# The first modulation of a transformer block: from split matmuls over weight rows to plain fp32 matmuls over weight columns, with part of the columns on VectorE

## The chip, the cores and the metric

The kernel runs on one core of one Trainium2 chip. The metric is the device time of one execution in microseconds (us); a comparison uses the median of several runs. The engines are named as the profile names them: PE (TensorE, the matmul engine), PEld (its weight loads), DVE (VectorE), ACT (ScalarE), POOL (GpSimd), SP (the engine that issues most of the DMA transfers).

## The reference, cut to what matters

The network is two blocks, one behind the other, on 256 tokens of width 1024. The first block works on two token streams (the latent one, `x`, and a context one, `ctx`, 512 tokens in all) and its first step scales and shifts every channel by values that come from a condition vector, one for each stream:

```
mod_lat = split(silu(c) @ w_mod[i] + b_mod[i], 6)
mod_ctx = split(silu(c_ctx) @ w_mod[i] + b_mod[i], 6)
u_ctx = h_ctx * (1 + mod_ctx[1]) + mod_ctx[0]
u_lat = h_lat * (1 + mod_lat[1]) + mod_lat[0]
y_ctx, y_lat = mla_mixer(u_ctx, u_lat, ...)
```

For the first layer the shift (part 0) and the scale (part 1) are needed before anything else can be multiplied: a product of two vectors of 1024 values with a matrix of 1024 x 2048 fp32 weights, 8 MB. All other modulation columns are needed later.

## The kernel before, in words

The kernel is one long program; a scheduler fixes the order of instructions on each engine when it is built, and each engine then works through its own list in that order and waits where data or a buffer is missing. Products of full fp32 weights are made by `mm3`: each operand is cut by `split` (line 117) into a rounded part `hi` (a cast, ACT, line 122) and a rest `lo` (a subtraction, DVE, line 123), and three matmuls (lines 156 to 158) go over hi x hi, hi x lo and lo x hi.

`first_in` (line 575) is the first stage. ACT starts four transfers of token rows (`xin`, line 581). PE transposes them (line 588), ACT copies the result to `xraw` (line 589); this is the function `mid`. `mod_first` makes the scale and shift as columns `mods[1]` and `mods[0]`, channel by channel on the partitions. Four units u of 512 weight columns each arrive as two transfers of 1 MB (line 134), are cut into hi and lo, and are the moving operand of 16 matmuls of 512 columns, with the 4 columns of `c4` (the two condition vectors, hi and lo) stationary. The result lies in 4 rows; ACT copies it (line 252) and 4 tiny matmuls turn it into columns (line 254). Units 0 and 1 give the first half of shift and scale, units 2 and 3 the second; after units 1 and 3 `use(b, ...)` applies them to the channels k = 4b to 4b+3: two `tensor_scalar` on DVE (line 598), one for each stream, then `split` into `xh` and `xl`, the operand of everything that follows.

What follows is the attention's input projection: first the unit `kr` (24 matmuls of 512 columns, tile `g<-xh,hi` and its two partners, weights `in_mla_in_kr`), then three units `in_mla_in` (tiles `acc`). Its weights pass the same `split`, so the casts and subtractions of `kr` stand between those of `use(1)` in the lists of ACT and DVE.

The modulation columns that are needed later are made on DVE alone by `mod_tick` (line 269): `crow[s]` holds silu of a condition vector on all partitions, a tile `mraw` of 128 weight columns lies transposed, and one `scalar_tensor_tensor` with an accumulated sum (line 278) gives one column for one stream.

Buffers: `wr` has 2 buffers `raw`, the phase 3 more; `mraw` has 3; `u` has 2.

Of the kernel before, what the change touches and what calls it, by code (L numbers as in the profile page):

```python
# [8 lines left out]
F32 = mybir.dt.float32  # L9
F32R = mybir.dt.float32r  # L10
I32 = mybir.dt.int32
AF = mybir.ActivationFunctionType
ALU = mybir.AluOpType
AX = mybir.AxisListType

P = 128
D = 1024
KD = D // P
T = 256
# [11 lines left out]
class Net:  # L31
# [198 lines left out]
        nc.scalar.dma_start(self.lncol, a["ln_cols"])  # L230

    def mod_first(self, mid, use):
        nc = self.nc
        pm = self.gen()
        sel = self.ft([4, 2], "msel")
        nc.scalar.dma_start(sel, self.a["k_sel42"])
        c4 = self.ft([P, KD, 4], "c4", 1, F32R)
        self.split(self.cT, c4[:, :, 0:2], c4[:, :, 2:4], "v")
        mods = [self.cp.tile([P, KD, 2], F32, name=f"mod0{c}") for c in range(2)]
        for u in range(4):  # L240
            ps = self.gen()
            for hf in range(2):
                raw = self.ft([P, 4 * 512], "raw", 3) if hf else None
                for i, W in enumerate(self.wload(self.a["w_mod0"][u, :, 4 * hf:4 * hf + 4, :], 4, 512, raw=raw)):
                    for j in range(2):
                        k = 4 * hf + 2 * i + j
                        for p, w in enumerate(W):
                            nc.tensor.matmul(ps[0:4, :], c4[:, k, :], w[:, j, :], start=k + p == 0, stop=k + p == KD)
            if u == 0:
                mid()  # L250
            r = self.mp.tile([P, D], F32, tag="mraw", name=self.nm("mrow"), bufs=3)[0:4, 0:512]
            nc.scalar.copy(r, ps[0:4, :])
            for j in range(4):
                nc.tensor.matmul(pm[:, 8 * u + 2 * j:8 * u + 2 * j + 2], r[:, j * P:(j + 1) * P], sel,
                                 start=True, stop=True)
            ch, b = u % 2, u // 2
            m = mods[ch][:, 4 * b:4 * b + 4, :]
            nc.vector.tensor_tensor(m, pm[:, 8 * u:8 * u + 8].rearrange("p (k s) -> p k s", s=2),
                                    self.bmod[:, 0, ch, 4 * b:4 * b + 4].unsqueeze(2).to_broadcast([P, 4, 2]), ALU.add)
            if ch:  # L260
                nc.vector.tensor_scalar(m, m, 1.0, None, ALU.add)
                use(b, mods[1], mods[0])

    def mod_start(self, i, ch, streams=(0, 1)):
        m = self.cp.tile([P, KD, 2], F32, tag="modcol", name=self.nm("modcol"), bufs=8)
# [309 lines left out]
    def first_in(self):  # L575
        nc, a = self.nc, self.a
        with self.phase("l0a"):
            raw = self.ft([P, KD, 512], "xraw")
            xs = [self.ft([P, D], "xin", 4) for _ in range(4)]
            for s in range(4):  # L580
                nc.scalar.dma_start(xs[s], a["x" if s > 1 else "ctx"][(s % 2) * P:(s % 2) * P + P])

            def mid():
                for s in range(4):
                    for b in range(0, KD, 4):
                        pt = self.trp()
                        for j in range(4):
                            nc.tensor.transpose(pt[:, j * P:(j + 1) * P], xs[s][:, (b + j) * P:(b + j + 1) * P], self.ident)
                        nc.scalar.copy(raw[:, b:b + 4, s * P:(s + 1) * P], pt.rearrange("p (j t) -> p j t", j=4))

            xT = self.new_xT(512)

            def use(b, A, B):
                for k in range(4 * b, 4 * b + 4):
                    u = self.ft([P, 512], "u", 2)
                    for s in range(2):
                        sl = slice(256 * (1 - s), 256 * (1 - s) + 256)
                        nc.vector.tensor_scalar(u[:, sl], raw[:, k, sl], A[:, k, s:s + 1], B[:, k, s:s + 1],
                                                ALU.mult, ALU.add)
                    self.split(u, xT[0][:, k, :], xT[1][:, k, :])  # L600

            self.mod_first(mid, use)
        return xT

    def layer0(self, stk):
        nc, a = self.nc, self.a
        sid = [1, 1, 0, 0]
        xT = self.first_in()
        self.crow = [self.mp.tile([P, D], F32, name=f"crow{i}") for i in range(2)]
        for r, src in zip(self.crow, (a["c"][0], a["c_ctx"])):  # L610
            nc.scalar.dma_start(r, src.unsqueeze(0).to_broadcast([P, D]))
            nc.scalar.activation(r, r, AF.Silu)
        j2 = self.mod_start(0, 2)
        j3 = self.mod_start(0, 3)
        j45 = []
# [1029 lines left out]
def constants():  # L1645
    k = {}
# [4 lines left out]
    for lv in range(7):  # L1651
        b = 1 << lv
        m = (tt // (2 * b)) * 2 * b + b
# [5 lines left out]
    j = (t % 32)[:, None]  # L1659
    i = np.arange(32)[None, :]  # L1660
    for lv in range(5):
        b = 1 << lv
# [4 lines left out]
    ti = np.arange(32)[None, :]  # L1667
    k["k_gneg"] = np.concatenate([np.where(m, -60000.0, 0.0) for m in (tt < tp, tt > tp, ti < tp % 32, ti > tp % 32)]
                                 + [tp != tt], axis=1).astype(np.float32)
    k["k_sel42"] = np.tile(np.eye(2, dtype=np.float32), (2, 1))  # L1670
    k["k_bsel"] = (np.arange(64) % 32 >= 16).astype(np.float32)[:, None]
    f = (t % 32 < 16).astype(np.float32)
    k["k_pmask"] = np.ascontiguousarray(np.stack([f, 1.0 - f], axis=1))
# [2 lines left out]
    pm = np.zeros((P, P), np.float32)  # L1676
# [13 lines left out]
def kblocks(w, n):  # L1690
    w = np.asarray(w)
    lead = w.shape[:-2]
    k, f = w.shape[-2] // P, w.shape[-1] // n
    w = w.reshape(*lead, k, P, f, n)
    r = len(lead)
    return np.ascontiguousarray(np.moveaxis(w, (r + 2, r + 1, r), (r, r + 1, r + 2)))
# [23 lines left out]
def layout1(x):  # L1720
    o = {}
    c = np.stack([np.asarray(x["c"])[0], np.asarray(x["c_ctx"])])
# [3 lines left out]
    for n in ("ln1_g", "ln1_b", "ln2_g", "ln2_b", "mla_q_norm", "mla_kv_norm"):  # L1726
        o[n] = np.asarray(x[n])
    w = np.asarray(x["w_mod"])
    o["w_mod0"] = kblocks(w[0, :, :2 * D], 512)[[0, 2, 1, 3]]
    w = np.concatenate([w[0, :, 2 * D:], w[1]], axis=1).reshape(KD, P, 10, D)  # L1730
    o["w_modb"] = np.ascontiguousarray(w.reshape(D, 10, KD, P).transpose(1, 2, 3, 0))
    o["c"] = np.asarray(x["c"])
# [1 line left out]
    w = np.asarray(x["mla_w_in"])[0]  # L1734
    o["mla_in"] = kblocks(w[:, :768], 256)
    o["mla_in_kr"] = kblocks(np.concatenate([w[:, 768:], w[:, 768:]], axis=1), P)[0]
    w = np.asarray(x["mla_w_q_up"])[0].reshape(512, 8, 192)
    o["mla_q_nope"] = tblocks(w[:, :, :P].reshape(512, D), 4)
    o["mla_q_rope"] = tblocks(w[:, :, P:].reshape(512, 512), 4)[0]
    w = np.asarray(x["mla_w_kv_up"])[0].reshape(256, 8, 256)  # L1740
# [3 lines left out]
    w = np.asarray(x["w_ffn_in"])  # L1744
# [3 lines left out]
    w = np.asarray(x["w_ffn_out"])  # L1748
    o["w_ffd0"] = rblocks(w[0], 2)
    o["w_ffd1"] = rblocks(w[1], 2)  # L1750
    w = np.asarray(x["gdn_w_in"])[0]
# [87 lines left out]
```

## Time and profile before

| | before |
|---|---|
| median of 3 runs (lowest, highest) | 2515.39 us (2508.4, 2516.76) |
| profiled execution, first to last instruction (span) | 2511.5 us |
| profiled execution's own time outside the span | not listed apart; the span is 3.9 us below the runs' median |
| PE busy, share of the span | 2350.2 us, 94% |
| DVE busy | 1767.2 us, 70% |
| ACT busy | 1258.2 us, 50% |

The busy share of PE is that of its records: a matmul counts from start to modelled end. The stage of which the change is a part is only about the first 50 us; how it stands there must be read from that stage's own rows, not from these shares.

### The profile page before, as it was taken

To read this page: it belongs to the slowest core of one execution; us is meant where nothing else is said; L and a number is where in the kernel's file an instruction comes from. 1 tells how busy PE (TensorE), PEld (TensorE's weight loads), DVE (VectorE), ACT (ScalarE), POOL (GpSimd) and SP (SyncE) were. 2 spreads that over 40 slices of the span, in tenths; PEclk is the share of its full clock that TensorE was granted. 3 is DMA by queue.
4 is the path that set the end of the run, shared out by engine and by line. 5 is a ranking of instruction groups with operands and counts; after the bars stand their busy time and mean duration, and the time that the engine had idled before them with its cause. 6 is when DMAs were issued, how large, how long until landed. Compare 5 with 4: busy or idle time off the path is not lost.

```text
span 2511.5 us, 38451 instructions
## 1 busy us (share of the span) xinstructions
PE 2350.2 (94%) x14526; PEld 1934.9 (77%) x14526; DVE 1767.2 (70%) x3380; ACT 1258.2 (50%) x2644; POOL 198.2 (8%) x264
## 2 busy tenths in 40 slices
PE   7999999999788999879799999999999999999998
PEld 4978878878677878768688778767788788767886
DVE  6886898965679979886655755577655555687554
ACT  6475432222375575645444555564645554665553
POOL 0000500000221021111300000001000000001000
PEclk9999999999989989989899999998999999998999
DMA  8544266641122121221655555432555455414552
GB/s 301 194 140 167 99 211 208 224 141 51 58 80 77 35 69 34 81 88 45 231 195 174 166 193 173 167 124 66 189 183 185 155 174 191 139 56 135 185 185 100
DMA packets 93634, 356.12 MB, mean 142 GB/s; under 512 B 12264, under 2 KB 13448, under 8 KB 86664
## 3 DMA queue, kind: packets, MB, share of 16 engines
q1 hardware_dynamic: 88544, 343.91, 41.4%
q10 hardware_dynamic: 3592, 6.02, 0.7%
q0 software_dynamic: 1312, 3.74, 0.4%
q8 instruction: 114, 1.87, 0.3%
q14 instruction: 72, 0.59, 0.1%
HBM read 348.77 MB, written 3.67 MB: 140 GB/s over the span
## 4 chain that ended last, share of the span: by engine, by line
PE 72%; DVE 13%; ACT 6%; DMA 4%; issue 3%; POOL 2%; ACTq 0%; DVEq 0%; POOLq 0%; SPq 0%
PE g L156 12%; PE g L158 12%; PE g L157 12%; PE acc L156 8%; PE acc L158 8%; PE acc L157 8%; DVE lo L123 2%; ACT hi L122 1%; DVE cvy L762 1%; DMA raw<-in_w_gu 1%; POOL t L163 1%; PE t L1288 1%; PE g L494 1%; PE acc L1514 1%; PE acc L996 1%
## 5 line engine op out<-in xcount | busy, mean ns | idle before, releaser
L122 ACT CAST hi<-raw 128x512 fp32r<-128x512 f32 (+3 forms) x740 | 488.8, 700 | 477.7 <-PE g L157 116.5
L123 DVE TENSOR_TENSOR lo<-raw,hi 128x512 fp32r<-128x512 f32 (+3 forms) x740 | 561.5, 791 | 205.5 <-ACT hi L122 199.3
L156 PE MATMUL g<-hi,xh 128*128 128x512 f32 (+1 forms) x1120 | 421.4, 376 | 14.1 <-DVE hid L1280 6.5
L158 PE MATMUL g<-hi,xl 128*128 128x512 f32 (+1 forms) x1120 | 410.2, 366 | 6.1 <-DVE xl L1245 4.8
L157 PE MATMUL g<-lo,xh 128*128 128x512 f32 (+1 forms) x1120 | 410.8, 367 | 1.2 <-DVE lo L123 1.2
L156 PE MATMUL g<-xh,hi 128*128 128x512 f32 (+1 forms) x776 | 280.9, 362 | 4.7 <-ACT cvu L758 4.7
L158 PE MATMUL g<-xh,lo 128*128 128x512 f32 (+1 forms) x776 | 279.0, 360 | 1.4 <-DVE lo L123 1.4
L157 PE MATMUL g<-xl,hi 128*128 128x512 f32 (+1 forms) x776 | 279.4, 360 | 0.0
L156 PEld LDWEIGHTS g<-hi,xh 128*128 128x128 f32 x1120 | 213.1, 190 | 52.7 <-DVE hid L1280 8.8
L158 PEld LDWEIGHTS g<-hi,xl 128*128 128x128 f32 x1120 | 212.7, 190 | 44.9 <-DVE xl L1245 5.7
L157 PEld LDWEIGHTS g<-lo,xh 128*128 128x128 f32 x1120 | 213.2, 190 | 34.6 <-DVE lo L123 2.1
L156 PE MATMUL acc<-xh,hh 128*128 128x512 f32 x440 | 176.1, 400 | 3.3 <-ACT hh L122 3.3
L123 DVE TENSOR_TENSOR xl<-raw,xh 128x512 fp32r<-128x512 f32 (+1 forms) x223 | 153.1, 698 | 30.2 <-ACT xh L122 30.2
L157 PE MATMUL acc<-xl,hh 128*128 128x512 f32 x440 | 172.9, 393 | 0.0
L158 PE MATMUL acc<-xh,hl 128*128 128x512 f32 x440 | 172.8, 397 | 0.0
L156 PEld LDWEIGHTS g<-xh,hi 128*128 128x128 f32 x776 | 151.0, 195 | 25.2 <-ACT cvu L758 5.6
L158 PEld LDWEIGHTS g<-xh,lo 128*128 128x128 f32 x776 | 150.6, 194 | 20.9 <-DVE lo L123 1.6
L157 PEld LDWEIGHTS g<-xl,hi 128*128 128x128 f32 x776 | 150.9, 195 | 18.7
L158 PE MATMUL acc<-hi,xl 128*128 128x512 f32 (+2 forms) x432 | 158.5, 370 | 4.6 <-DVE xl L1245 3.3
L1280 DVE SCALAR_TENSOR_TENSOR hid<-g,t,hid 128x256 f32<-128x256 f32 (+1 forms) x96 | 44.3, 461 | 167.8 <-ACT hid L1279 167.6
L157 PE MATMUL acc<-lo,xh 128*128 128x512 f32 (+2 forms) x432 | 159.4, 371 | 2.1 <-DVE lo L123 2.1
L156 PE MATMUL acc<-hi,xh 128*128 128x512 f32 (+2 forms) x432 | 160.6, 376 | 0.2 <-ACT hi L122 0.2
(567 smaller groups left out, 4152.5 us busy)
## 6 DMA issues: line engine op xcount, KB each, us to landing
raw<-in_w_gu SPq DMA_DIRECT2D x220, 512.0 KB, 4.4
raw<-in_w_down SPq DMA_DIRECT2D x88, 512.0 KB, 4.4
mraw<-in_w_modb SPq DMA_DIRECT2D x80, 512.0 KB, 4.5
raw<-in_w_in SPq DMA_DIRECT2D x28, 512.0 KB, 4.0
raw<-in_w_ffg SPq DMA_DIRECT2D x11, 1024.0 KB, 5.0
raw<-in_w_ffu SPq DMA_DIRECT2D x11, 1024.0 KB, 4.9
raw<-in_w_ffd SPq DMA_DIRECT2D x11, 1024.0 KB, 4.8
raw<-in_w_ffd SPq DMA_DIRECT2D x22, 512.0 KB, 4.3
```

Source lines behind the costliest of these rows:

```text
L122: nc.scalar.copy(hi, src)
L123: self.tail = nc.vector.tensor_tensor(lo, src, hi.bitcast(F32), ALU.subtract).ins
L156: nc.tensor.matmul(out, lh, rh, start=start, stop=False)
L157: nc.tensor.matmul(out, lh, rl, start=False, stop=False)
L158: nc.tensor.matmul(out, ll, rh, start=False, stop=stop)
L163: self.pow = self.nc.gpsimd.tensor_tensor(dst, s, self.mhalf[:, 0:n], ALU.pow).ins
L494: nc.tensor.matmul(po[:, tt * P:(tt + 1) * P], v[:, j, h * P:(h + 1) * P], PT[:, j * P:(j + 1) * P], start=j == 0, stop=j == nk // P - 1)
L762: nc.vector.scalar_tensor_tensor(y, u[:, :, j:j + T], w[:, j:j + 1], y, ALU.mult, ALU.add)
L996: nc.tensor.matmul(py[:, vh * P:(vh + 1) * P], Mt[:, 4 * (4 * d + vh) + c, :], src[:, vh, :], start=True, stop=True)
L1280: nc.vector.scalar_tensor_tensor(h, v, r, h, ALU.mult, ALU.mult)
L1288: nc.tensor.transpose(pt[:, j * P:(j + 1) * P], hid[:, j * P:(j + 1) * P], self.ident)
L1514: nc.tensor.matmul(pcv[s][:, ct * P:(ct + 1) * P], self.upad[:, ct, s * P + j:s * P + j + P], dg, start=ct + j == 0, stop=False)
```

## The change

The same 2048 columns are made in two ways. All 1024 scale columns and the last 256 shift columns go to PE as five units of 256 columns (`on_pe`, 1 MB each): the fp32 weights, uncut, are the stationary operand, block by block of 128 x 128, and the moving operand is `cT`, 2 columns. The result is at once in columns, in one PSUM tile `pm`. The first 768 shift columns go to DVE as six tiles of 128 (`on_dve`, 0.5 MB each), in the way of `mod_tick`. For this `crow` is loaded and passed through silu at the start instead of after the stage. No `split` of these weights, no copy of rows and no tiny matmuls are left; `+1` and the bias become one instruction. In `use`, the stream s = 1 is now scaled on ACT instead of DVE.

```diff
     def mod_first(self, mid, use):
-        c4 = self.ft([P, KD, 4], "c4", 1, F32R)
-        self.split(self.cT, c4[:, :, 0:2], c4[:, :, 2:4], "v")
...
-        for u in range(4):
-            ps = self.gen()
-            for hf in range(2):
-                raw = self.ft([P, 4 * 512], "raw", 3) if hf else None
-                for i, W in enumerate(self.wload(self.a["w_mod0"][u, :, 4 * hf:4 * hf + 4, :], 4, 512, raw=raw)):
-                    for j in range(2):
-                        k = 4 * hf + 2 * i + j
-                        for p, w in enumerate(W):
-                            nc.tensor.matmul(ps[0:4, :], c4[:, k, :], w[:, j, :], start=k + p == 0, stop=k + p == KD)
...
+        self.crow = [self.mp.tile([P, D], F32, name=f"crow{i}") for i in range(2)]
+        for r, src in zip(self.crow, (a["c"][0], a["c_ctx"])):
+            nc.scalar.dma_start(r, src.unsqueeze(0).to_broadcast([P, D]))
+            nc.scalar.activation(r, r, AF.Silu)
+        pm = self.gen()[:, 0:4 * KD].rearrange("p (c k s) -> p c k s", c=2, k=KD)
...
+        def on_pe(u, ch, j0):
+            raw = self.ft([P, KD, T], "raw", 3) if u % 2 else self.wr.tile([P, KD, T], F32, tag="raw", name=self.nm("raw"))
+            nc.sync.dma_start(raw, a["w_mod0"][u])
+            for j in range(2):
+                for k in range(KD):
+                    nc.tensor.matmul(pm[:, ch, j0 + j, :], raw[:, k, j * P:(j + 1) * P], self.cT[:, k, :],
+                                     start=k == 0, stop=k == KD - 1)
+
+        def on_dve(j):
+            raw = self.mp.tile([P, D], F32, tag="mraw", name=self.nm("mraw"), bufs=3)
+            nc.sync.dma_start(raw, a["w_mods"][j])
+            for s in range(2):
+                junk = self.mp.tile([P, D], F32, tag="mjunk", name=self.nm("mjunk"), bufs=1)
+                nc.vector.scalar_tensor_tensor(junk, raw, 1.0, self.crow[s], ALU.mult, ALU.mult,
+                                               accum_out=mods[0][:, j, s:s + 1])
+
+        def add(b, ch, j0, j1):
...
+            nc.vector.scalar_tensor_tensor(mods[ch][:, sl, :], src, float(ch), bias, ALU.add, ALU.add)
+
+        on_pe(0, 1, 0)
+        on_dve(0)
+        on_dve(1)
+        mid()
+        on_pe(1, 1, 2)
+        on_dve(2)
+        on_dve(3)
+        add(0, 1, 0, 4)
+        add(0, 0, 0, 4)
+        use(0, mods[1], mods[0])
+        on_pe(2, 1, 4)
+        on_dve(4)
+        on_pe(3, 1, 6)
+        on_dve(5)
+        on_pe(4, 0, 6)
+        add(1, 1, 4, 8)
+        add(1, 0, 4, 6)
+        add(1, 0, 6, 8)
+        use(1, mods[1], mods[0])
```

and in `use`:

```diff
-                        nc.vector.tensor_scalar(u[:, sl], raw[:, k, sl], A[:, k, s:s + 1], B[:, k, s:s + 1],
-                                                ALU.mult, ALU.add)
+                        Ak, Bk = A[:, k, s:s + 1], B[:, k, s:s + 1]
+                        if s:
+                            nc.scalar.activation(u[:, sl], raw[:, k, sl], AF.Identity, bias=Bk, scale=Ak)
+                        else:
+                            nc.vector.tensor_scalar(u[:, sl], raw[:, k, sl], Ak, Bk, ALU.mult, ALU.add)
```

**PE's list.** Before, in the first stage (transposes at line 588, matmuls with moving `hi` and `lo` and the four stationary columns `c4` at line 248, which the rows call `c_15`, and the tiny matmuls at line 254), around the end of unit 0:

```order
L248 MATMUL g_126<-hi_151,c_15_121 4x512
L248 MATMUL g_126<-lo_152,c_15_121 4x512
L588 MATMUL t_175<-ident,xin_109 128x128 x4
L588 MATMUL t_181<-ident,xin_109 128x128 x4
L588 MATMUL t_187<-ident,xin_110 128x128 x4
L588 MATMUL t_193<-ident,xin_110 128x128 x4
L254 MATMUL g_118<-msel_119,mrow_211 128x2 x4
L248 MATMUL g_218<-hi_221,c_15_121 4x512
```

PE's list of the change from its first matmul to the unit `kr` (transposes now line 607, the new matmuls line 246):

```order
L607 MATMUL t_157<-ident,xin_108 128x128 x2
L246 MATMUL g_124<-csT,raw_127 128x2 x16
L607 MATMUL t_157<-ident,xin_108 128x128 x2
L607 MATMUL t_163<-ident,xin_108 128x128 x4
L246 MATMUL g_124<-csT,raw_205 128x2 x16
L607 MATMUL t_169<-ident,xin_109 128x128 x4
L607 MATMUL t_175<-ident,xin_109 128x128 x4
L607 MATMUL t_181<-ident,xin_110 128x128 x4
L607 MATMUL t_187<-ident,xin_110 128x128 x4
L246 MATMUL g_124<-csT,raw_257 128x2 x14
L607 MATMUL t_193<-ident,xin_111 128x128 x4
L607 MATMUL t_199<-ident,xin_111 128x128 x4
```

Behind these rows stand the last 2 matmuls of `raw_257`, 16 of `raw_281` and 16 of `raw_305`, and then `kr`. The 64 matmuls of 512 columns and the 16 tiny ones are gone, 80 matmuls of 2 columns have come.

**DVE's list.** Before, it begins with the cut of the condition vectors and then has the rests of the weights, in the order of their transfers:

```order
L120 CAST c_15_121<-csT 128x8x2
L123 TENSOR_TENSOR c_15_121<-csT,c_15_121 128x8x2
L123 TENSOR_TENSOR lo_130<-raw_127,hi_129 128x1024
L123 TENSOR_TENSOR lo_134<-raw_127,hi_133 128x1024
L123 TENSOR_TENSOR lo_148<-raw_145,hi_147 128x1024
```

In the change it begins with the addition of the bias to the first four scale columns, which PE makes from `raw_127` and `raw_205`; the sums over weights (line 254) stand behind it:

```order
L261 SCALAR_TENSOR_TENSOR mod_126<-g_124,bmod 128x8
L254 SCALAR_TENSOR_TENSOR mjunk_147,mod_125<-mraw_145,crow_118 128x1024
L254 SCALAR_TENSOR_TENSOR mjunk_149,mod_125<-mraw_145,crow_119 128x1024
L254 SCALAR_TENSOR_TENSOR mjunk_153,mod_125<-mraw_151,crow_118 128x1024
L254 SCALAR_TENSOR_TENSOR mjunk_155,mod_125<-mraw_151,crow_119 128x1024
L254 SCALAR_TENSOR_TENSOR mjunk_225,mod_125<-mraw_223,crow_118 128x1024
```

So all of DVE's work of the stage now stands behind PE's second unit. Further down DVE's list of the change, at the second `use` (line 261 adds, line 621 scales, line 123 cuts; `raw_366` is the weight of `kr`):

```order
L254 SCALAR_TENSOR_TENSOR mjunk_303,mod_125<-mraw_299,crow_119 128x1024
L261 SCALAR_TENSOR_TENSOR mod_126<-g_124,bmod 128x8
L261 SCALAR_TENSOR_TENSOR mod_125<-mod_125,bmod 128x4
L261 SCALAR_TENSOR_TENSOR mod_125<-g_124,bmod 128x4
L621 TENSOR_SCALAR u_326<-xraw_107,mod_126,mod_125 128x256
L621 TENSOR_SCALAR u_331<-xraw_107,mod_126,mod_125 128x256
L123 TENSOR_TENSOR lo_369<-raw_366,hi_368 128x1024
L123 TENSOR_TENSOR xl_117<-u_326,xh_116 128x512
```

The three additions read what PE made from `raw_257`, `raw_281` and `raw_305`; the cut of `kr`'s weight, which its third matmul needs, stands behind them.

## Rows read from the trace of the kernel before

**Rows 1.** The page's head.
```profile
span 2511.5 us, 38451 instructions
```

**Rows 2.** Windows: length, busy PE, PEld, DVE, ACT, POOL, granted clock, DMA share, GB/s.
```profile
10.00:20.00 10.00, 6.20 (x24) 3.17 (x25) 6.65 (x7) 6.27 (x8) 0.00 (x0) 1.00 1.02 421
...
60.00:80.00 20.00, 19.16 (x162) 18.96 (x161) 18.43 (x29) 7.00 (x16) 1.52 (x2) 1.00 0.64 211
```

**Rows 3.** PE's timeline: start, length, line, tiles, count [idle before, releaser].
```profile
13.80 1.94 PE L588 MATMUL t<-ident,xin 128*128 128x128 f32 x8 [13.80 <-DMA xin<-in_ctx]
15.39 0.78 PE L248 MATMUL g<-hi,c 128*4 128x512 f32 x1
...
21.50 1.15 PE L588 MATMUL t<-ident,xin 128*128 128x128 f32 x8 [0.24 <-ACT xraw L589]
...
45.57 0.79 PE L158 MATMUL g<-xh,lo 128*128 128x512 f32 x1 [1.43 <-DVE lo L123]
```

**Rows 4.** Groups of instructions from 0 to 52 us: busy, mean ns.
```profile
L123 DVE TENSOR_TENSOR lo<-raw,hi 128x1024 fp32r<-128x1024 f32 x19 | 22.5, 1218 | 9.8 <-ACT hi L122 9.8
L122 ACT CAST hi<-raw 128x1024 fp32r<-128x1024 f32 x19 | 18.8, 1045 | 4.3 <-issue 4.1 <-DMA raw<-in_w_mod 0.2
...
L248 PE MATMUL g<-lo,c 128*4 128x512 f32 x32 | 13.1, 408 | 0.3 <-DVE lo L123 0.3
...
L254 PE MATMUL g<-msel,mrow 4*128 4x2 f32 x32 | 4.2, 249 | 2.8 <-ACT mrow L252 2.8
```

**Rows 5.** A DMA list: the first `xin` transfer, issued at 2.15 us; last, landing time.
```profile
xin<-in_ctx ACTq DMA_DIRECT2D x1, 512.0 KB, 11.5
```

**Rows 6.** DVE's timeline around the second `use` and the first later column.
```profile
42.79 0.17 DVE L261 TENSOR_SCALAR mod<-mod 128x8 f32<-128x8 f32 x1
43.00 1.38 DVE L598 TENSOR_SCALAR u<-xraw,mod,mod 128x256 f32<-128x256 f32 x4
...
45.44 1.28 DVE L123 TENSOR_TENSOR xl<-u,xh 128x512 fp32r<-128x512 f32 x2
...
62.58 1.22 DVE L278 SCALAR_TENSOR_TENSOR mjunk<-mraw,crow 128x1024 f32<-128x1024 f32 x1
...
63.83 1.22 DVE L278 SCALAR_TENSOR_TENSOR mjunk<-mraw,crow 128x1024 f32<-128x1024 f32 x1
```

**Rows 7.** The only plain fp32 matmuls of 128x128 weights and 2 columns.
```profile
L916 PE MATMUL t<-ones,half 128*128 128x2 f32 x32 | 3.9, 236 | 0.0
```

**Rows 8.** PE's timeline of short matmuls in two later stretches.
```profile
1709.25 3.62 PE L1514 MATMUL acc<-cdg,upad 128*128 128x128 f32 x16
1712.66 2.58 PE L1562 MATMUL g<-sv,halfA 128*128 128x64 f32 x16
...
2249.95 1.91 PE L1562 MATMUL g<-sv,halfA 128*128 128x64 f32 x16
2251.70 1.06 PE L1574 MATMUL g<-gv,gla_AT 128*128 128x64 f32 x8
```

**Rows 9.** PEld's timeline (weight loads) of the first of these stretches.
```profile
1712.45 1.75 PEld L1562 LDWEIGHTS g<-sv,halfA 128*128 128x128 f32 x8
```

**Rows 10.** Windows as in group 2, of four later stretches and the restart at 45 us.
```profile
894.90:911.90 17.00, 17.00 (x304) 12.47 (x304) 13.42 (x21) 7.93 (x14) 0.73 (x1) 0.50 0.11 34
1707.20:1714.10 6.90, 6.90 (x81) 6.66 (x81) 6.66 (x11) 4.30 (x17) 1.49 (x4) 0.51 0.01 2
1720.70:1724.10 3.40, 3.40 (x147) 2.65 (x133) 2.65 (x6) 1.31 (x6) 1.10 (x2) 1.00 0.02 5
1724.30:1731.10 6.80, 6.80 (x31) 6.09 (x30) 6.62 (x11) 1.18 (x7) 0.73 (x1) 0.50 0.27 82
45.00:51.70 6.70, 6.13 (x14) 4.79 (x15) 6.70 (x12) 2.22 (x4) 0.00 (x0) 0.50 0.56 195
```

**Rows 11.** PE's timeline: what stands in the first and third stretch of group 10.
```profile
894.23 0.44 PE L1116 MATMUL acc<-big,Mt 32*32 32x32 f32 x16 [1.16 <-DVE Mt L944]
...
1720.37 0.52 PE L1528 MATMUL g<-m_E 32*32 32x32 f32 x38
```

More of the change, by code (lines that the diff above doesn't have):

```diff
@@ L232, in mod_first @@
     def mod_first(self, mid, use):
[L233 to L236, printed above, removed]
-        c4 = self.ft([P, KD, 4], "c4", 1, F32R)
-        self.split(self.cT, c4[:, :, 0:2], c4[:, :, 2:4], "v")
-        mods = [self.cp.tile([P, KD, 2], F32, name=f"mod0{c}") for c in range(2)]
-        for u in range(4):
-            ps = self.gen()
-            for hf in range(2):
-                raw = self.ft([P, 4 * 512], "raw", 3) if hf else None
-                for i, W in enumerate(self.wload(self.a["w_mod0"][u, :, 4 * hf:4 * hf + 4, :], 4, 512, raw=raw)):
-                    for j in range(2):
-                        k = 4 * hf + 2 * i + j
-                        for p, w in enumerate(W):
-                            nc.tensor.matmul(ps[0:4, :], c4[:, k, :], w[:, j, :], start=k + p == 0, stop=k + p == KD)
[L249 to L262, printed above, removed]
@@ new lines, in mod_first @@
+        nc, a = self.nc, self.a
+        self.crow = [self.mp.tile([P, D], F32, name=f"crow{i}") for i in range(2)]
[3 more added lines that the diff above has]
+        pm = self.gen()[:, 0:4 * KD].rearrange("p (c k s) -> p c k s", c=2, k=KD)
+        mods = [self.cp.tile([P, KD, 2], F32, name=f"mod0{c}") for c in range(2)]
+        def on_pe(u, ch, j0):
[5 more added lines that the diff above has]
+                                     start=k == 0, stop=k == KD - 1)
@@ new lines, in on_dve @@
+        def on_dve(j):
[6 more added lines that the diff above has]
+        def add(b, ch, j0, j1):
+            sl = slice(j0, j1)
+            bias = self.bmod[:, 0, ch, sl].unsqueeze(2).to_broadcast([P, j1 - j0, 2])
+            src = pm[:, ch, sl, :] if ch or j0 == 6 else mods[0][:, sl, :]
+            nc.vector.scalar_tensor_tensor(mods[ch][:, sl, :], src, float(ch), bias, ALU.add, ALU.add)
@@ L608, in layer0 @@
         xT = self.first_in()
[L609 to L612, printed above, removed]
         j2 = self.mod_start(0, 2)
@@ L1669, in constants @@
                                  + [tp != tt], axis=1).astype(np.float32)
-    k["k_sel42"] = np.tile(np.eye(2, dtype=np.float32), (2, 1))
     k["k_bsel"] = (np.arange(64) % 32 >= 16).astype(np.float32)[:, None]
@@ L1728, in layout1 @@
     w = np.asarray(x["w_mod"])
-    o["w_mod0"] = kblocks(w[0, :, :2 * D], 512)[[0, 2, 1, 3]]
+    o["w_mod0"] = kblocks(np.concatenate([w[0, :, D:2 * D], w[0, :, D - 256:D]], axis=1), 256)
+    o["w_mods"] = np.ascontiguousarray(w[0, :, :D - 256].T.reshape(6, P, D))
     w = np.concatenate([w[0, :, 2 * D:], w[1]], axis=1).reshape(KD, P, 10, D)
```

## The prediction

> **What bounds the kernel now.** I read the page first, for the span [rows 1], then the windows, to see how full PE is once the network proper runs: 19.16 of 20 us between 60 and 80 us, and it stays so [rows 2]. From there on PE is the bound, and whatever moves the start of that dense work moves the end by the same amount. So the question is when the dense work begins. In PE's timeline that is the third matmul of `kr`, at 45.57 us, released by DVE's cut of `kr`'s weight; the two matmuls ahead of it are done by then, and behind it PE does not wait again for long [rows 3]. Next I read the groups of the first 52 us to see what fills them: on ACT and DVE the casts and subtractions of the weights, 1.045 and 1.218 us each, 19 of each, of which 16 are of `w_mod` [rows 4]. DVE is the last link before the restart: it adds the bias, scales, and then cuts `kr`'s weight [rows 6]. Of PE the reader should see that it is fed and not full in this stage, and that its moving operand is wide, 512 columns.
>
> **What the change removes.** On ACT 16 casts, 16.7 us, and on DVE 16 subtractions, 19.5 us [rows 4]. On PE 64 matmuls of 512 columns (0.41 us each in their records) and the 16 tiny ones [rows 4]. That these 16 stand as 32 in the row shows that a plain fp32 matmul is two instructions on PE; line 916 shows the same for the form that is now added [rows 4, 7].
>
> **What it adds on PE.** 80 matmuls of 128x128 weights and 2 columns are thus 160 pairs of weight load and matmul, beside the 32 transposes as before: 192 instructions one behind the other. What one costs is the disputed price. With few columns the weight load sets the pace: 16 with 64 columns start 1.75 us before the next group at the full clock, 0.109 us each [rows 8], and 32 with 2 columns were busy 3.9 us, 0.122 each [rows 7]. At the low clock (granted 0.51, [rows 10]) 16 with 128 columns take from 1709.25 to 1712.66, 0.213 each [rows 8], and with 64 columns the loads still stand about 0.22 apart (8 in 1.75 us, [rows 9]): fewer columns save nothing, and the load slows with the clock. [...]
>
> [...]
>
> **Which clock.** PE begins cold: the first 8 transposes start 1.59 us before the matmul that follows them, 0.20 us each, which is the slow pace (the granted clock reads as full there, the pace does not) [rows 3]. Before, the 512-column matmuls behind them soon run at the full clock. In the change there is no wide matmul until `kr`. [...] From 894.9 to 911.9 us PE was busy 17.00 of 17.00 us, with many 32x32 matmuls between wide ones, and stayed at 0.50 the whole time; from 1720.7 to 1724.1 it was busy throughout with such small ones at the full clock, and the next stretch was granted 0.50 [rows 10, 11]. A full PE list is thus not enough. Against this, the clock came back at 1714.1 out of matmuls of 128 and 64 columns at the slow pace [rows 8, 10]. [...]
>
> [...]
>
> **The sum.** PE's first instruction waits for the first `xin`, issued at 2.15 us and landed 11.5 us later; PE began at 13.80 [rows 3, 5]. In the change SP's list has 2 MB instead of 3 ahead of or beside it, because the second and third transfers are 0.5 MB; at 421 GB/s [rows 2] that is 2.4 us less, 11.4. Bounds 11.3 and 13.8; I take 12.0. PE's list then needs 40.9 us, and some waits for ACT's copies between transposes, as the 0.24 us before [rows 3]: three of them, 0.7 us (bounds 0 and 1.5). PE is through at 53.6 us. Behind it on DVE wait three additions at 0.17, two scalings at 0.35 (four in 1.38) and the cut of `kr`'s weight, 1.22 [rows 4, 6]: 2.4 us, so the third matmul of `kr` can start at 56.0 instead of 45.57: **10.4 us later**. By the bounds 9.0 to 13.1.
>
> The restart itself I take as costing the same: before, PE ran at 0.50 from 45.0 to 51.7 us [rows 10]; in the change it also comes out of the low clock. If that lasts some 3 us less, 1.5 us come back. The sum on the profiled span is 2511.5 + 10.4 = 2521.9; the runs' median lies 3.9 us above this span, and on it the forecast is 2515.4 + 10.4 = **2526 us**.
>
> **What is hidden.** DVE's list begins with an addition that waits for PE's second unit: 72 instructions, 15.3 us, so 27.3 us. From there 12 sums at 1.25 (62.58 to 63.83) are 15.0, and with the first `use` (four scalings 1.4, four cuts 2.6) and two additions DVE is ready at 46.7, 6.9 us before PE [rows 6]. If that cover goes, DVE sets the end; see the first rival. `crow` is the fifth and sixth transfer in ACT's queue: with 3 MB there and at most 5.5 MB of weights beside it, 8.5 MB at 421 GB/s [rows 2] end at about 23 us, 1 us for silu, before the 27.3 at which DVE asks. The scaling that moves to ACT and the ACT time freed lie beside DVE. `mraw` is held by the sums, so SP's later transfers wait for DVE, but the last weight for PE (`raw_305`) goes out after the fourth sum, about 32 us, 14 us before PE comes to it. `in_mla_in` goes out when PE lets go of the `wr` buffer, about 53.6, while `kr` still needs 24 matmuls.
>
> **Rival 1, not slower: the short matmuls run at the full pace.** Its place is PE's list, its price 192 x 0.109 to 0.122 instead of 0.213, and it decides below a mean of 0.198 us, where the delay falls under 7.5 us. Then PE is through at about 35 us and DVE sets the end. Its list begins between 20.3 us (PE's second unit) and 25 (`crow`), say 22.5; 15.0 for the sums, 4.2 for additions and the first `use`, 2.4 for the rest: the cut of `kr` ends at 44.1, 1.5 us earlier than before. Time 2514, between 2512 and 2516.5. For it: line 916's row; against it: the 17 us at 0.50.
>
> **Rival 2: the delay is given back later.** The work behind the stage would have to have slack. PE had 0.84 us of it in 60 to 80 us, DVE 1.57 [rows 2]: taken off the 10.4 they leave 8.0, time 2523.4, and off the lower bound of 9.0 they leave 6.6, time 2522, within 0.3%. Low-clock stretches further down, such as that of 6.8 us [rows 10], can also fall otherwise; one more or less is some 3 us either way.
>
> **Rival 3: PE starts late and waits more.** With 13.8 us and 1.5 us of waits the delay is 13.1, time 2528.5, and one more slow stretch makes 2531.
>
> **Faster** by over 0.3% (7.5 us, about what runs of this kernel can tell from no change) would need DVE's list to begin at 16.5 us, ahead of PE's second unit even at the full clock; only later stretches could do it.
>
> **The numbers.** The slow clock holds the stage: 0.84, of which 0.71 come out above 7.5 us and 0.13 below, for rivals 2 and 3 and the bounds. Rival 1: 0.12, nearly all of it within 0.3%. What is left, 0.04, goes to either side. Slower 0.71, within 0.3% 0.25, faster 0.04. The likeliest case's own range is 2521 to 2530; with rival 1 taken in as far as 2 in 10 demand it is 2514 to 2531.
>
> **What would show it.** After: the groups of line 246 with 160 records; their starts 0.21 us apart (right) or 0.11 (wrong: rival 1); the third matmul of `kr` near 56 us, released by DVE's cut, and DVE waiting for PE ahead of the second `use`. If DVE runs up to that point without a wait, or waits there for `crow` or `mraw`, the hidden part was misjudged. If the start is late as forecast and the end is not, rival 2 holds.

## The result, and the profile after the change

The changed kernel takes 2536.33 us (median; 2525.58 to 2540.72 over 5 runs) against 2515.39 us (2508.4 to 2524.05 over 5 runs) before: ratio 1.0072, 95% interval 1.0051 to 1.0092, which is 18 us slower, between 13 and 23. The forecast of 2526 us had the direction and too small a size; the median lies 5 us above the range's upper end. The profiled execution is the shortest of its runs, 1.8 us outside its span:

```profile
span 2523.8 us, 38569 instructions
```

Against the 2511.5 us of [rows 1] its span is 12.3 us longer. First the stage itself, in PE's timeline (columns as in [rows 3]; line 607 are the transposes, line 246 the new matmuls, lines 156 to 158 `kr`):

```profile
10.85 0.66 PE L607 MATMUL t<-ident,xin 128*128 128x128 f32 x2 [10.85 <-DMA xin<-in_ctx]
11.30 6.83 PE L246 MATMUL g<-csT,raw 128*128 128x2 f32 x32
17.98 1.52 PE L607 MATMUL t<-ident,xin 128*128 128x128 f32 x6
19.30 6.83 PE L246 MATMUL g<-csT,raw 128*128 128x2 f32 x32
25.98 3.74 PE L607 MATMUL t<-ident,xin 128*128 128x128 f32 x16
29.51 3.35 PE L246 MATMUL g<-csT,raw 128*128 128x2 f32 x28
32.72 1.46 PE L607 MATMUL t<-ident,xin 128*128 128x128 f32 x8
33.98 14.51 PE L246 MATMUL g<-csT,raw 128*128 128x2 f32 x68
48.34 0.78 PE L156 MATMUL g<-xh,hi 128*128 128x512 f32 x1
48.91 0.63 PE L157 MATMUL g<-xl,hi 128*128 128x512 f32 x1
50.72 0.80 PE L158 MATMUL g<-xh,lo 128*128 128x512 f32 x1 [1.18 <-DVE lo L123]
```

PE works without a gap from 10.85 to 48.34 us. The first two groups of 32 records take 6.68 us from their start to the next group, 0.21 each, and so do the last 68; only the 28 that begin at 29.51, behind 16 transposes, run at 0.115. The third matmul of `kr` starts at 50.72, 5.15 us later than in [rows 3]. DVE's timeline (sums at line 254, additions at 261) says who is late:

```profile
26.16 0.17 DVE L261 SCALAR_TENSOR_TENSOR mod<-g,bmod 128x8 f32<-128x8 f32 x1 [26.16 <-PE g L246]
...
43.67 1.22 DVE L254 SCALAR_TENSOR_TENSOR mjunk<-mraw,crow 128x1024 f32<-128x1024 f32 x1
48.52 0.17 DVE L261 SCALAR_TENSOR_TENSOR mod<-g,bmod 128x8 f32<-128x8 f32 x1 [3.63 <-PE g L246]
...
49.45 1.22 DVE L123 TENSOR_TENSOR lo<-raw,hi 128x1024 fp32r<-128x1024 f32 x1
```

It starts when PE's second unit is done, is through with its sums at 44.9, stands 3.63 us for PE, and needs 2.4 us from there to the cut of `kr`'s weight. The windows (as in [rows 2, 10]) show the low clock from the middle of the stage into `kr`, and the dense work behind it as full as before:

```profile
60.00:80.00 20.00, 19.11 (x160) 18.90 (x159) 17.07 (x25) 5.69 (x13) 1.22 (x2) 1.00 0.75 267
33.30:53.70 20.40, 19.23 (x82) 17.95 (x81) 16.67 (x36) 11.19 (x20) 0.00 (x0) 0.50 0.72 265
```

Of the low clock only 3 us lie behind `kr`'s third matmul, where before they were 6, so `kr`'s last matmul starts at 56.99 for 53.72, and behind it the dense work is 4.0 us late. That is a third of the 12.3 us by which the profiled span grew. The order of the instructions behind the stage is the same in both kernels, so each can be laid beside its partner; the delay of PE's starts (median over 50 us of the run) against the kernel before is my own reckoning from the two traces:

```
at us of before     60    300   600   850   1150  2500
changed kernel      4.0   5.2   7.8   13.2  17.3  12.5
```

So two thirds of this execution's loss arise far behind the change. What waits there is seen in PE's waits from 780 to 1260 us that end in nothing the profile names (us in total, times, longest). Before:

```profile
PE acc L1116 <- issue: 0.6, 1, 0.6
PE t L1116 <- issue: 0.5, 1, 0.5
PE g L1116 <- issue: 0.2, 1, 0.2
```

After (line 1134 is the line 1116 of before):

```profile
PE acc L1134 <- issue: 5.4, 3, 2.5
PE acc L158 <- issue: 2.6, 1, 2.6
```

1.3 us have become 8.0. These stand in stretches of 32x32 matmuls, some 10 ns apart.

### The profile page after: what moved, and what is told of

It reads as the page before. It is cut to its first block, busy times and chain, and to the rows that moved or that the text cites. A ratio compares the mean times of both kernels' runs of the same rounds, so it can differ in the third digit from the quotient of the medians.

```text
span 2523.8 us, 38569 instructions
## 1 busy us (share of the span) xinstructions
PE 2360.8 (94%) x14590; PEld 1957.3 (78%) x14590; DVE 1759.8 (70%) x3377; ACT 1245.6 (49%) x2632; POOL 197.1 (8%) x264
## 4 chain that ended last, share of the span: by engine, by line
PE 72%; DVE 13%; ACT 6%; DMA 4%; issue 3%; POOL 2%; ACTq 0%; DVEq 0%; POOLq 0%; SPq 0%
PE g L156 12%; PE g L157 12%; PE g L158 12%; PE acc L156 8%; PE acc L157 7%; PE acc L158 7%; DVE lo L123 2%; ACT hi L122 1%; DMA raw<-in_w_gu 1%; PE g L246 1%; DVE cvy L780 1%; POOL t L163 1%; DMA raw<-in_w_ffg 1%; PE t L1306 1%; PE g L513 1%
## 5 line engine op out<-in xcount | busy, mean ns | idle before, releaser
L122 ACT CAST hi<-raw 128x512 fp32r<-128x512 f32 (+3 forms) x724 | 472.9, 693 | 466.7 <-PE g L157 111.7
L123 DVE TENSOR_TENSOR lo<-raw,hi 128x512 fp32r<-128x512 f32 (+3 forms) x724 | 542.5, 783 | 192.7 <-ACT hi L122 186.4
```

Source lines behind the costliest of these rows:

```text
L122: nc.scalar.copy(hi, src)
L123: self.tail = nc.vector.tensor_tensor(lo, src, hi.bitcast(F32), ALU.subtract).ins
```

## The experiments

**Theory 1**: the start is late, and the shifted run loses more behind it, by low-clock stretches that fall otherwise. **Theory 2**: a late start costs its delay and no more; the rest is chance of single runs. The first four kernels set them against each other; all shared the runs of the kernel before (median 2516.47 us).

**The changed kernel again**, no edit. 

> The changed kernel once more, nothing edited. Its first profile put the third matmul of kr 5.15 us later than before (50.72 for 45.57 us), while the medians differ by 20.9 us; about 12 us of the profiled execution's loss arise behind the stage. Theory 1 (the later loss belongs to the change, because all that follows runs shifted and the low-clock stretches fall otherwise): again 15 to 21 us over the kernel before, and in a second trace the delay against before grows at the same places, near 800 and 1140 us. Theory 2 (5 us from the stage, the rest chance of the runs): 4 to 12 us this time, and the low-clock stretches of the second trace lie otherwise than in the first.

Measured: 2532.35 us, ratio 1.0056 (1.0037 to 1.0075). The loss is real, and its second trace is worse in the stage:

```profile
29.63 5.97 PE L246 MATMUL g<-csT,raw 128*128 128x2 f32 x28
...
51.58 0.77 PE L156 MATMUL g<-xh,hi 128*128 128x512 f32 x1
...
53.95 0.80 PE L158 MATMUL g<-xh,lo 128*128 128x512 f32 x1 [1.18 <-DVE lo L123]
```

The 28 records that were fast in the first trace are slow here: 40.6 us from 10.96 to 51.58 for 192 instructions, 0.21 each throughout; `kr` is 8.4 us late. The issue waits are there again, in the same places:

```profile
PE acc L1134 <- issue: 6.0, 3, 2.5
PE acc L158 <- issue: 2.3, 1, 2.3
```

**A pure delay**, the kernel before with

```diff
                 nc.vector.tensor_scalar(m, m, 1.0, None, ALU.add)
+                if u == 3:
+                    late = self.acc1()
+                    for i in range(28):
+                        nc.tensor.matmul(late[:, 2 * i:2 * i + 2], self.ident, m[:, 3, :], start=True, stop=True)
```

> The kernel before with a pure delay: 28 plain fp32 matmuls of the identity with 2 columns (56 instructions, their result not read) on PE ahead of kr, nothing else moved. The third matmul of kr comes 4 to 6 us later. Theory 1 (a late start of the dense work brings further losses behind it): 12 to 20 us slower than before. Theory 2 (the loss of the stage is all that a late start costs): 4 to 6 us slower.

Measured: 2535.47 us, ratio 1.0069 (1.0051 to 1.0087).

```profile
45.53 9.61 PE L265 MATMUL acc<-mod,ident 128*128 128x2 f32 x56 [0.46 <-DVE mod L261]
```

The 56 records took 9.5 us to the next start, 0.17 each, nearer to the 0.21 of the stage above than to the 0.109 of [rows 8], so the delay came out larger than the 4 to 6 us expected; 2.5 us of it stood there before they began, since the addition of [rows 6] is at 45.30 for 42.79. At 60 us of the run the delay is 9.1 us, at 850 us 17.4. So 17 us (13 to 22) for a delay of 9: more than theory 2 allows. **Twice as many** (`range(56)`):

> The same pure delay twice as long: 56 such matmuls, 112 instructions, 12 to 13 us of them at the full pace and 24 us at the low one; part lies in time in which PE waited for DVE before. The third matmul of kr comes 10 to 20 us later. Theory 2: the end is later by the same amount as that matmul, within 4 us. Theory 1: it is later by 7 us or more beyond it.

Measured: 2544.01 us, ratio 1.01 (1.008 to 1.012), 25 us for a delay of 20.0.

```profile
43.61 22.39 PE L265 MATMUL acc<-mod,ident 128*128 128x2 f32 x112 [0.46 <-DVE mod L261]
```

The excess is 5 us here (0 to 10) and was 8 there (4 to 13). It does not seem to grow with the delay, as theory 1 would have it, but each is the difference between the medians of several runs and the delay of one trace, and the 0 to 10 still hold the 7 us or more that theory 1 asked for. These two runs alone do not settle it.

**Wide matmuls among the narrow ones**, the changed kernel with

```diff
...
-                    nc.tensor.matmul(pm[:, ch, j0 + j, :], raw[:, k, j * P:(j + 1) * P], self.cT[:, k, :],
-                                     start=k == 0, stop=k == KD - 1)
+                    mm = nc.tensor.matmul(pm[:, ch, j0 + j, :], raw[:, k, j * P:(j + 1) * P], self.cT[:, k, :],
+                                          start=k == 0, stop=k == KD - 1)
+                    if k % 3:
+                        with self.tc.issue_after(mm.ins):
+                            nc.tensor.matmul(wide, wt[:, 0:P], wt, start=True, stop=True)
```

Ahead of this `wt` is made, a tile of 512 columns, and `wide`, the tile for the result, which is not read.

> The changed kernel with 50 wide matmuls added (one pass, 512 columns, result not read) behind two of three of the narrow ones. If the narrow ones are slow because no wide work holds the clock up, the granted clock is full through most of the stage, the narrow records are 0.11 us each, PE is through at 42 to 45 us in spite of 50 more matmuls, DVE (ready at about 46) becomes the last link, and the third matmul of kr starts at 47 to 48.5 us instead of 50.7. If the low clock has another cause, PE is through only at 55 to 60 us. For the end: theory 2 gives the kernel before plus 2 to 3 us in the first case; theory 1 leaves it open (plus 2 to 15 us), by where the low-clock stretches then fall.

Measured: 2550.57 us, ratio 1.0128 (1.0107 to 1.0149). The remedy failed, and both times expected for the end of PE's part were too early. From PE's timeline:

```profile
15.90 0.85 PE L250 MATMUL g<-csT,raw 128*128 128x2 f32 x4
16.60 0.77 PE L254 MATMUL acc<-widet 128*128 128x512 f32 x1
17.18 0.85 PE L250 MATMUL g<-csT,raw 128*128 128x2 f32 x4
...
73.58 0.63 PE L156 MATMUL g<-xh,hi 128*128 128x512 f32 x1
```

Four narrow ones take 0.70 us to the next start and a wide one 0.58, where four at the 0.109 of [rows 8] are 0.44 and the last matmuls of `kr` before follow each other by 0.23; and so it stays to the end of the stage, although the granted clock reads 1.00 from 11 to 70 us: 50 wide matmuls, almost half of PE's time, did not bring the faster pace. `kr` is 29.8 us late, the end 32 (27 to 38).

**What the five traces share.** Numbering PE's instructions in the order of the traces (weight loads, matmuls, recorded waits), I found that the long issue waits, where a kernel has them, lie at the same numbers, 8641, 8897, 10689, 12737 and 15041, which differ by multiples of 256, while the work that stands there differs: the change puts 126 instructions more ahead of it, the delays 112 and 224. That made **theory 3**: PE stops at borders of blocks of 256 instructions when it comes to one too early, and the number of instructions ahead decides which work a border cuts. The page has a transfer queue of that kind, the same in the kernel before:

```profile
q8 instruction: 114, 1.87, 0.3%
```

114 packets of 16.4 KB for the 29,346 instructions of PE in the changed kernel's trace and the 29,220 in that of before, one for each 256 of them. At the first stop of the changed kernel, PE's timeline and then this queue between 815.7 and 817.3 us:

```profile
815.88 0.20 PE L1134 MATMUL acc<-big,xv 32*32 32x32 f32 x2
818.59 0.26 PE L1134 MATMUL acc<-xv,big 32*32 32x32 f32 x1 [2.52 <-issue]
```

```profile
q8 instruction: 1, 0.02, 5.7%
```

One packet, 815.75 to 817.20 us: it begins 1.2 us after PE crossed the border ahead, at 814.59, and PE goes on 1.4 us behind its end.

The next four tested this, beside a kernel before of 2517.36 us. **Count alone**: the kernel before with tiny matmuls in PE's idle start, 32 and 64 of them (128 and 256 instructions), and the changed kernel with 32:

```diff
+            cnt = self.acc1()
+            for i in range(32):
+                nc.tensor.matmul(cnt[0:32, 4 * i:4 * i + 4], self.ident[0:32, 0:32], self.ident[0:32, 0:4], start=True, stop=True)
+
             def mid():
```

> The kernel before with 32 tiny matmuls (32 rows, 4 columns, 128 instructions of PE with their weight loads, result not read) added in the time in which PE waits for the first token rows; the start of kr stays within 0.5 us. Theory 3, new: in all six traces the longest waits of PE marked issue in the stretches of small matmuls lie at the same numbers of its list (8641, 8897, 10689, 12737, 15041, which differ by multiples of 256), whatever the time; so PE stops at certain numbers of its list, and a change of the count of instructions ahead (126 more in the changed kernel) decides which work stands there. By theory 3 this kernel gets the stalls of the changed one (2.7, 2.0 to 2.5, 1.2 and 2.4 us at these numbers) and is 3 to 8 us slower than before. By theories 1 and 2 it is within 3 us of it, since nothing starts later.

> The same with 64 tiny matmuls, 256 instructions: theory 3 puts the same work at the same numbers as before, less one block, so no new stalls and a time within 3 us of before, less than that with 128. If the added matmuls cost by themselves (a colder or later PE), it is slower than the one with 128.

> The changed kernel with the 32 tiny matmuls in the idle start: 126 and 128 make 254, so the work stands at nearly the numbers of before. Theory 3: the stalls at 8897, 10689, 12737 and 15041 go, and it is 4 to 8 us faster than the changed kernel, 8 to 13 us slower than before. Theories 1 and 2: as the changed kernel, 15 to 21 us slower than before.

Measured: before with 128: 2527.41 us, ratio 1.0054 (1.0035 to 1.0073), 14 us slower by 9 to 18. Before with 256: 2512.27 us, 0.9986 (0.9975 to 0.9997). Changed with 128: 2525.15 us, 1.0039 (1.0022 to 1.0055), 10 us slower than before (5.5 to 13.8) where the changed kernel alone is 14 (9 to 19) and 18 (13 to 23). PE's issue waits from 780 to 1260 us, first of the kernel before with 128:

```profile
PE acc L1120 <- issue: 4.4, 3, 2.0
PE acc L158 <- issue: 3.3, 1, 3.3
```

and of the changed kernel with 128, whose long stops are gone:

```profile
PE acc L1138 <- issue: 0.4, 1, 0.4
```

In the kernel before the 128 added instructions stand from 2.61 to 6.18 us, where PE waited for `xin` anyway; yet it loses nearly as much as the changed kernel. But its trace is not free of a delay:

```profile
2.61 3.57 PE L585 MATMUL acc<-ident 32*32 32x4 f32 x64 [2.61 <-DMA ident<-in_k_ident]
...
23.95 0.87 PE L254 MATMUL g<-msel,mrow 4*128 4x2 f32 x4 [1.79 <-DMA msel<-in_k_sel]
...
50.86 0.50 PE L158 MATMUL g<-xh,lo 128*128 128x512 f32 x1 [1.43 <-DVE lo L123]
```

PE stood 1.79 us for `msel`, an operand of the tiny matmuls, and in the last unit its matmuls of 512 columns were still 0.43 us apart at 43.73 us, and 0.23 only from 44.58 on (before: 0.23 in that unit from its start at 36.31), so the third matmul of `kr` came 5.3 us late where 0.5 was expected; at 60 us of the run the delay is 4.0. Whether the other runs of this kernel had it, no profile shows. The run therefore leaves theory 2 some 4 of its 14 us, and theory 1 more; cleaner is the count of 64 below, whose stage is as before's. By numbers in PE's list, my own count from the traces: the longest gap between two starts at each border / the time of the 250 instructions ahead of it, us:

```
kernel            added  8641       8897       10689      12737      15041
before                0  0.74/2.47  0.03/4.49  0.10/6.19  0.22/3.22  0.73/4.30
before, 16 tiny      63  0.34/2.70  0.05/4.19  2.12/2.07  2.07/1.25  1.08/3.68
before, delay 28    112  0.12/2.82  2.43/1.28  1.82/2.07  2.13/1.25  0.45/2.57
changed             126  0.32/2.82  2.71/1.26  2.02/1.25  1.24/1.26  2.64/1.25
changed again       126  0.27/2.83  2.71/1.27  2.55/1.50  1.33/1.26  2.38/2.07
before, 32 tiny     127  0.31/2.83  2.16/1.26  1.80/1.25  1.05/1.24  3.45/1.25
before, delay 56    224  0.03/3.05  2.70/1.26  0.00/4.61  0.01/3.54  1.73/1.26
changed, 32 tiny    253  0.02/2.89  0.58/2.46  0.01/3.78  0.02/4.20  0.01/2.08
before, 64 tiny     255  0.02/3.11  0.57/2.48  0.00/6.21  0.02/4.44  0.01/1.33
weights moving        6  0.49/2.48  0.05/4.71  0.05/5.85  0.13/3.07  0.49/4.27
```

Nearly always a block that was worked off in 1.3 us is followed by a stop of 1 to 3.5 us, one that took 2.1 by 1.8 to 2.4, one that took 2.4 to 2.9 by 0.8 or less, one that took over 3 by next to none (0.49, 0.73 and 1.08 at 15041 are the exceptions). The last column also has two fast blocks without a stop, for which I have no reason. The packet tells more than the pace: each of the 20 stops of 1 us or more in the table ends 1.2 to 1.6 us behind the end of the instruction queue's packet that belongs to that border (the packets counted from the start of the run).

**The weights as moving operand**, the changed kernel with

```diff
+            ps = self.gen()[0:2, 0:T]
+            for k in range(KD):
+                nc.tensor.matmul(ps, self.cT[:, k, :], raw[:, k, :], start=k == 0, stop=k == KD - 1)
+            r = self.ft([2, T], "mrow", 2)
+            nc.scalar.copy(r, ps)
             for j in range(2):
-                for k in range(KD):
-                    nc.tensor.matmul(pm[:, ch, j0 + j, :], raw[:, k, j * P:(j + 1) * P], self.cT[:, k, :],
-                                     start=k == 0, stop=k == KD - 1)
+                nc.tensor.matmul(pm[:, ch, j0 + j, :], r[:, j * P:(j + 1) * P], self.ident[0:2, 0:2],
+                                 start=True, stop=True)
```

> The changed kernel with the plain fp32 weights as the moving operand (256 columns, the 2 columns of the condition stationary), the rows of the result copied by ACT and turned into columns by 10 tiny matmuls; DVE's and ACT's other work as in the change. [...] If plain fp32 is slow in itself whatever moves, PE is through no earlier than 48 us. The count of PE's instructions is within 10 of before: by theory 3 there are no added stalls and the end is within 5 us of before; by theory 1 a start 2 us late still costs 7 us or more.

Measured: 2518.08 us, ratio 1.001 (0.9998 to 1.0022): the loss is gone.

```profile
11.91 5.38 PE L246 MATMUL g<-raw,csT 128*2 128x256 f32 x16
...
24.27 1.14 PE L611 MATMUL t<-ident,xin 128*128 128x128 f32 x8 [3.82 <-ACT xraw L612]
...
43.32 3.62 PE L246 MATMUL g<-raw,csT 128*2 128x256 f32 x16
47.39 0.60 PE L250 MATMUL g<-ident,mrow 2*128 2x2 f32 x4 [0.45 <-ACT mrow L248]
...
50.23 0.80 PE L158 MATMUL g<-xh,lo 128*128 128x512 f32 x1 [1.57 <-DVE lo L123]
```

A unit is 16 records at 0.226 us instead of 32 at 0.21, so 3.6 us for 6.7; part of that is PE's pace, since the same 16 records of the first unit here took 5.3 us to the next start, at 17.22, 0.33 each. PE was through only at 47.9 us, mostly because PE stood 4.7 us for ACT, which waited for `crow` before it copied `xraw`. `kr` is 4.7 us late, and behind it 3.5; the end is 2.5 us (-0.5 to 5.5) behind before.

The last four sought a better version and more points for theory 3; three of them stood beside a kernel before of 2518.0 us. **`crow` requested earlier** (behind the first `xin`), and on top of that **PE's last unit on DVE** as two more tiles:

```diff
...
             for s in range(4):
                 nc.scalar.dma_start(xs[s], a["x" if s > 1 else "ctx"][(s % 2) * P:(s % 2) * P + P])
+                if s == 0:
+                    for r, src in zip(self.crow, (a["c"][0], a["c_ctx"])):
+                        nc.scalar.dma_start(r, src.unsqueeze(0).to_broadcast([P, D]))
...
```

```diff
...
-        on_pe(4, 0, 6)
+        on_dve(6)
+        on_dve(7)
...
```

> As the kernel with the weights moving, and the two rows of the condition (crow) requested behind the first xin instead of behind the fourth. There PE stood 3.8 and 0.9 us because ACT, which works in order, waited for crow before it copied xraw, and PE was through at 47.9 us. Without that PE is through at 42 to 44 us and the third matmul of kr starts at 43 to 46, before's 45.6 or somewhat earlier; the count of PE's instructions is as in that kernel, so no added stalls (theory 3): within 5 us of before, likelier below it. If the request only changes the order in which transfers share the memory's rate, PE's start is later by 1 to 2.5 us and the gain is half.

> As the one above, but the last unit of PE (256 shift columns) goes to DVE as two more tiles: four units on PE, eight tiles on DVE. PE's list is 5 us shorter, DVE's 2.6 us longer by two tiles of two sums less the additions. If PE still ends the stage above, the third matmul of kr comes 2 to 4 us earlier than there; if DVE does, later by 2 to 5. Theory 3: 40 instructions fewer on PE, a place in the list with 1 to 2 us more of stalls than before.

Measured: 2516.28 us, ratio 1.0001 (0.9986 to 1.0017), and 2528.82 us, 1.0044 (1.0028 to 1.006). The starts of `kr`'s third matmul, first with `crow` earlier, then with the unit moved:

```profile
45.90 0.40 PE L158 MATMUL g<-xh,lo 128*128 128x512 f32 x1
```

```profile
44.87 0.50 PE L158 MATMUL g<-xh,lo 128*128 128x512 f32 x1 [1.88 <-DVE lo L123]
```

The first gives before's start and before's time. The second starts `kr` earlier and still ends 11 us behind (7 to 15): DVE has put its last sums between the cuts, so the second half of `u` comes only from 51.8 us on and PE is 4.1 us late behind `kr`, and with 33 instructions fewer on PE a border cuts the small matmuls:

```profile
PE acc L1140 <- issue: 2.0, 1, 2.0
PE g L1140 <- issue: 1.5, 1, 1.5
```

Its runs also show a lower mean granted clock, 0.966 against 0.969 beside it. How its 11 us divide among the three I have not separated.

**The count between**, the kernel before with 16 tiny matmuls, and the one with 64 once more:

> The kernel before with 16 tiny matmuls, 64 instructions, in PE's idle start. From the traces so far a stop at a block's border is long when the block ahead of it was worked off fast: 1.3 us for 256 instructions gives stops of 1.1 to 3.5 us, 2.5 us gives 0.5 to 0.7, over 3 us gives under 0.5. With 3.3 us less the block's time for each stop, the borders moved by 64 sum to 5.4 us, by 128 to 7.4, by none to 2.7. Theory 3: this kernel is 1 to 5 us slower than before, less than that with 128. Theories 1 and 2: no change, within 3 us.

> The kernel before with 64 tiny matmuls (256 instructions) once more: it was the only one below before, by 0.14% with an interval that just leaves out no change. Theory 3 has no reason for a gain (the borders stand as before, the sum of stops 3.0 for 4.3 us in one trace each): within 3 us of before. If the gain is real, 3 to 7 us below it again.

Measured: 2526.08 us, ratio 1.0031 (1.0014 to 1.0049), 8 us slower (4 to 12), less than with 128 by the ratio as expected, though more than the 1 to 5 us that I had worked out; the stops are in the table. Its third matmul of `kr` starts 0.6 us later than in [rows 3]:

```profile
46.20 0.79 PE L158 MATMUL g<-xh,lo 128*128 128x512 f32 x1 [1.43 <-DVE lo L123]
```

The repeated one: 2516.13 us beside 2516.6, ratio 0.9997 (0.9985 to 1.0009). The small gain of its first measurement does not hold: moving all the borders' work by one whole block changes nothing, as theory 3 has it. At 60 us of the run PE's starts are 0.5 us behind before's in the trace with 64 instructions, and -0.1 and 0.4 in the two with 256. So the same kind of dummy, with the stage as it was, costs 8 us at one count and nothing at another; theories 1 and 2 have no room for that. Of the kernels that the table leaves out, the one with wide matmuls (226 added) stops 2.16 and 1.81 us at 8897 and 15041, the one with a unit moved (33 fewer) 2.16 us at 8641, and the others do not stop for over 0.7 us at the five borders. No version here beats the kernel before.

## Why the prediction came out as it did

The right parts. The pace of the narrow matmuls is 0.21 us, and PE, not DVE, ends the stage: in the second trace 192 instructions take 40.6 us, forecast 40.9, which was 192 at the 0.213 of [rows 8]; that this pace would hold for the whole stage was my estimate. The faster pace of rival 1 came for 28 records of the first profile, at 0.115 us, and for none of the second. In the first profile DVE began at 26.16 (forecast 27.3), was ready to within 2 us of the forecast, and waited for PE; 2.4 us from there to `kr` was 2.38. `crow` came at 25.7, 1.7 us later than forecast and still in time. `raw_305` went out at 31.8 (forecast 32).

Mis-sized in the stage, all to the early side: PE's start, 10.85 for 12.0, outside the bounds of 11.3 and 13.8; the waits between transposes, none for 0.7 us; in the first profile the pace rose once, for those 28 records at 0.115 us, which saved 3 us. So `kr` is 5.15 us late in one trace and 8.4 and 8.3 in the two others, for the 10.4 of the sum. Rival 1 is refuted but for those 28 records, and rival 3 too: PE began early and waited less.

**The step that failed** is the first: "whatever moves the start of that dense work moves the end by the same amount". The stage accounts for about half. With the count put right by 128 tiny matmuls the changed kernel is 10 us (5.5 to 13.8) behind before, which is its stage (8.3 us late in that trace); without them 14 and 18. The missing term is the stops at the borders of blocks of 256 instructions of PE, 8.9 and 9.2 us at the five borders of the table for 1.8 before. They are set off by the count, 126 more instructions on PE, and not by the delay, since 64 instructions that leave the stage as it was cost 4 to 12 us, and 256 nothing. The sum counted what every added instruction takes, and not what its number does to the work 800 us later.

Low-clock stretches, which I had named as the way in which the rest could move, have a share as well. In the 29 runs of the kernel before that stand beside the first test of the count, the nine with the lowest granted clock (0.968 on average) take 2519 us and the nine with the highest (0.973) 2512, about 1.4 us for 0.001 of the clock. The kernel before with 128 instructions has a mean clock 0.003 below before's, which by that is an estimated 4 of its 14 us, part of it perhaps in the stage, and the one with 64 has 0.0016 less, an estimated 3 of its 8 by the runs beside it (1.8 us for 0.001). Single traces do not always follow this: behind 100 us the low-clock stretches sum to 140.7 us in the trace of before, 144.0 and 174.9 in the two of the changed kernel, 148.3 in before with 128, some 161 in the changed one with 128, whose profiled run is 6 us above its median, and 154.8 in the second one of before with 256, whose span is the shortest of all, 2510.5 us. In the longer of the changed kernel's traces they may have a large share.

What stays open: the count alone costs somewhat more (14 us by 9 to 18, and 8 by 4 to 12) than its stops at these five borders sum to beyond before's (7.0 and 3.8). Other borders do not make up for it: over all borders, the stops that end just behind their packet sum to 3.2 us in the trace of before, 9.0 with 128 and 6.7 with 64. The lower clock could cover most of the rest, by the estimates above; why it is lower in these kernels, and whether the stops have to do with it, no run here tells. Nor was it tried to make the narrow matmuls themselves fast by anything but wide ones among them.

## What to carry to other kernels

A plain fp32 matmul with the weights stationary and 2 columns moving was two instructions of 0.21 us here, for the whole list in the second trace of the changed kernel and for all but 28 of them, at 0.115, in the first. With the operands turned round, so that the weights move, the same 8 products of 128x256 weights took 5.3 us in the first unit instead of 6.7, and 3.6 us in the last three. When the number of a kernel's PE instructions changes, look at the issue waits in stretches of small matmuls anywhere behind the change; a few dummy matmuls in idle time tell whether the loss is the change's own or that of its count: here 16 of them cost 8 us (4 to 12), and 64 nothing (ratio 0.9997). A result that hangs on this should be compared at a count that differs by a whole number of blocks, here of 256.

## What the runs showed of the hardware that I had not expected

PE works off 250 instructions of small matmuls in 1.25 us, 5 ns each, and at the next border it then stands: the four long stops of the changed kernel end 4.0, 3.3, 2.5 and 4.05 us after the border ahead, and in the kernel before with 128 3.46 us at the first. These stops end 1.2 to 1.4 us behind the end of the queue's packet of 256 instructions. At the five borders of the table the stops sum to 8.9 us in the changed kernel's first trace.

With 50 matmuls of 512 columns among the 2-column ones, almost half of PE's time, four narrow ones stayed at 0.70 us and a wide one at 0.58 to the end of the stage, some 60 us. In the first profile of the changed kernel the pace went from 0.21 to 0.115 us for 28 records behind 16 transposes in a row; in the second, with the same list, it did not: 0.21 for the same 28. The windows' granted clock reads 1.00 from 11.0 to 51.6 us of that second trace, though the pace is 0.21 all the time; there the pace is to be read, not the column.
